# Differential heads weighed in pairs: one run of 24 score matmuls and one pool of six PSUM banks

## Chip, cores and metric

The kernel runs on one core of one Trainium2 chip. The metric is the device time of one execution in microseconds (us). Before the change it is 2826.71 us, the median of 3 runs (2826.54 to 2827.23).

## What is computed

A bidirectional encoder of two layers over 256 tokens of width 2048, batch 1, all in float32. Each layer does this (shortened from the reference):

```
h = rmsnorm(x, g_mix[i]);  z = h @ w_in[i]
dq, dk, dv, cq, ckv, kr, ga, gb = split(z)

# A: differential attention, 8 heads, two maps of width 64 per head
scores  = einsum('bqhcd,bkhcd->bhcqk', dq, dk) * 64 ** -0.5
probs   = softmax(scores)
weights = probs[:, :, 0] - lam * probs[:, :, 1]
od      = rmsnorm(weights @ dv, g_subln[i]) * (1 - lam_init)

# B: latent attention, 8 heads: q from cq, k and v from ckv, a shared rotary key
om = softmax((q_nope k_nope + q_rope k_rope) * 192 ** -0.5) @ v_mla

m = sigmoid(ga) * (od @ w_branch_diff[i]) + sigmoid(gb) * (om @ w_branch_mla[i])
x = x + m @ w_out[i]
x = x + swiglu(rmsnorm(x)) ;  x = x + sigmoid(rmsnorm(x) @ w_ple_gate[i]) * (p[i] @ w_ple_in[i])
```

A last RMSNorm follows the two layers.

## The kernel before

**Products.** Nearly all the time goes into products of a 128-column strip of weights with the 256 tokens. A product (`product`, lines 227 to 236) has 16 chunks where its input is 2048 wide. For each chunk `emit` (216 to 225) issues two TensorE matmuls: line 219 takes the high part of the weights against 512 columns (the high and the low part of the input side by side), line 223 the low part against the 256 columns of the high part. The weights come by DMA in pieces of 128x1024; ScalarE rounds the high part out of a piece (`whi`, line 194) and VectorE subtracts it for the low part (`wlo`, also line 194, shown under line 76, the helper's). Three buffers of each part let the pieces run ahead of TensorE. A product accumulates in one PSUM bank of the pool `ps_mm`; ScalarE copies its second half out (`join`, line 249) and VectorE adds the first half to it (`joined`, 247 to 252). That add frees the bank.

**PSUM.** [...] Before the change `ps_mm` has four for the products, `ps_s` two for the scores, `ps_at` two for everything small (transposes, the products with the values, norms).

**The differential stage**, once per layer. For a head, `queries_keys` (563 to 571) makes a query and a key product, rotates and splits them. `scores` (413 to 422) then multiplies both maps of a head: a map is 64 wide, so its matmuls use 64 of the array's 128 rows, and the loop alternates between the maps, which lie on the two halves of the rows. Two maps, two query blocks and three terms (high and low parts) make 12 matmuls of 64x256 per head, into two banks. `exps` (424 to 432) reads each bank: a VectorE maximum, a small scaling, two ScalarE exponentials with their sums, a VectorE reciprocal. `diff_weights` (674 to 683) joins the two maps into one tile `E` of weights; `E` and `E1` have two buffers each. `diff_out` (685 to 696) transposes the weights on TensorE (`turned`, 434 to 445, line 439), copies them out, and multiplies by the values (line 691).

**Order.** `pipelined` (709 to 718) goes head by head: a step of the filling work, the scores and weights of head h+1, the transposes of head h, another step, the product with the values of head h. The filling work is the generator `beside` (616 to 636): the short products of `keys_up` (two chunks each, in pairs) in turn with `queries_keys` of heads 2 to 7, then `queries_up`, gates, and the norms of the heads (`settle`). The text is a program order only: a planner (the scheduler of the Tile framework) orders each engine's queue by that priority and by when it takes operands and buffers to be ready, and it puts later products on TensorE while earlier work waits. `tc.keep_in_program_order(m)` ties an instruction behind the one that was written before it for its engine. In a queue everything stays in the planned order.

The latent attention (`mla_weights`, 727 to 734) uses `scores` too, with one map of full height. The end of the kernel (926 to 944) transposes the result through banks of `ps_s`, `ps_mm` and `ps_at`.

Of the kernel before, what the change touches and what calls it, by code (L numbers as in the profile page):

```python
# [15 lines left out]
AF = mybir.ActivationFunctionType  # L16
ALU = mybir.AluOpType
AX = mybir.AxisListType

P = 128  # L20
T = 256
# [3 lines left out]
DH = 8  # L25
# [29 lines left out]
def encoder(ctx, tc, x, p, positions, cols, lams, wq, wk, wv, wcq, wckv, wkr, wga, wgb,  # L55
            w_q_up, w_kn, w_v, w_bd, w_bm, w_out, w_gate, w_up, w_down, w_pin, w_pg, rope_c, out):
    nc = tc.nc
    V, A, PE = nc.vector, nc.scalar, nc.tensor
    PSUM = bass.MemoryType.PSUM
    pool = lambda name, bufs=1, **k: ctx.enter_context(tc.tile_pool(name=name, bufs=bufs, **k))  # L60
# [1 line left out]
    wts = pool("wts")  # L62
    tmp = pool("tmp")
    stat = pool("stat")
    ps_mm = pool("ps_mm", 4, space=PSUM)
    ps_s = pool("ps_s", 2, space=PSUM)
    ps_at = pool("ps_at", 2, space=PSUM)

    def scratch(tag, bufs, n=T):
# [2 lines left out]
    def bank(ps=ps_at, tag="at", name="at", shape=(P, 2 * T)):  # L72
        return ps.tile(list(shape), F32, tag=tag, name=name)
# [4 lines left out]
    def stt(o, a, s, b, op0, op1):  # L78
        return V.scalar_tensor_tensor(out=o, in0=a, scalar=s, in1=b, op0=op0, op1=op1)

    def ts(o, a, s1, s2, op0, op1=ALU.bypass):
        return V.tensor_scalar(out=o, in0=a, scalar1=s1, scalar2=s2, op0=op0, op1=op1)  # L82
# [11 lines left out]
    def operand(t):  # L94
        return t.rearrange("p c t -> p (c t)")
# [24 lines left out]
    halves = rc[:, 4 : 4 + P]  # L120
# [28 lines left out]
    neg_lam = const.tile([P, DEPTH], F32, name="neg_lam")  # L149
    gsub = const.tile([P, DEPTH], F32, name="gsub")  # L150
    lam_s = const.tile([P, DEPTH, 2], F32, name="lam_s")
    lam_in = tmp.tile([P, 2, T], F32, tag="E", name="lam_in", bufs=2).rearrange("p l (f d) -> p l f d", f=4)

# [93 lines left out]
    def joined(acc, o=None):  # L247
        t = scratch("join", 3)
        A.activation(t, acc[:, T:], AF.Copy)  # L249
        o = scratch("a", 4) if o is None else o  # L250
        tt(o, acc[:, :T], t, ALU.add)
        return o
# [113 lines left out]
    krs = [const.tile([P, 2 * T], F32R, name=f"kr{j}") for j in range(2)]  # L366
# [26 lines left out]
    def narrow(src, us):  # L393
# [13 lines left out]
                PE.matmul(acc, both[:, j * P : (j + 1) * P], us[a + j], start=a + j == 0, stop=a + j == NC - 1)  # L407
        return acc

    def three(q, k):  # L410
        return [(q[:, :T], k[:, T:]), (q[:, T:], k[:, :T]), (q[:, :T], k[:, :T])]

    def scores(*maps):


        Ss = [bank(ps_s, "S", "S", (P, 2, T)) for _ in maps]
        for b in range(2):
            for j in range(len(maps[0])):
                for S, pairs in reversed(list(zip(Ss, maps))):
                    q, k = pairs[j]  # L420
                    PE.matmul(S[:, b, :], q[:, b * P : (b + 1) * P], k, start=j == 0, stop=j == len(pairs) - 1)  # L421
        return Ss

    def exps(S, E, scale):

        nm, sm, rs = (stat.tile([P, 2], F32, tag=t, name=t, bufs=4) for t in ("nm", "sm", "rsum"))
        V.tensor_reduce(out=nm, in_=S, axis=AX.X, op=ALU.max, negate=True)
        ts(nm, nm, scale, None, ALU.mult)
        for b in range(2):
            last_exp[0] = A.activation(E[:, b, :], S[:, b, :], AF.Exp, bias=nm[:, b : b + 1], scale=scale, accum_out=sm[:, b : b + 1])  # L430
        V.reciprocal(out=rs, in_=sm)
        return rs

    def turned(W, parts=False):

        tp = bank(shape=(P, 2, T))
        for kb in range(2):
            for b in range(2):
                PE.transpose(tp[:, kb, b * P : (b + 1) * P], W[:, b, kb * P : (kb + 1) * P], ident)  # L439
        wt = [tmp.tile([P, 2, T], F32R if parts else F32, tag="wt", name="wt", bufs=4) for _ in range(1 + parts)]  # L440
        A.activation(wt[0], tp, AF.Copy)
        if not parts:
            return wt[0]
        tt(wt[1], tp, wt[0].bitcast(F32), ALU.subtract)
        return wt

    def head(vals, kb, h):
        return vals[:, kb, h // 4, (h % 4) * P : (h % 4 + 1) * P]

    def weights(tag="E", dt=F32):  # L450
        return tmp.tile([P, 2, T], dt, tag=tag, name=tag, bufs=2)
# [65 lines left out]
    for L in range(DEPTH):  # L517
# [43 lines left out]
        qk = [(ub[h], operand(fa(h, F32R))) for h in range(DH)]  # L561
# [13 lines left out]
        qn, kn, qr = [], [], ub[14:]  # L575
# [40 lines left out]
        def beside():  # L616

            for h in range(2, DH):
                if h < 6:
                    keys_up(2 * h - 4)  # L620
                elif h == 7:
                    rotated(joined(narrow(wkr[L], ua)), crm, srm)
                yield
                queries_keys(h)
                yield
            for n in (8, 0, 2, 10):
                if n == 0:
                    settle(0)
                gate(wga, gate_a, next(todo))
                queries_up(n)  # L630
                yield
            settle(4)
            for n in (4, 6):
                gate(wga, gate_a, next(todo))
                queries_up(n)
            gate(wga, gate_a, next(todo))
# [33 lines left out]
        fill = beside()  # L670
        od, ods = [], ub[:8]
        ssd = stat.tile([P, 2 * DH], F32, tag="ssd", name="ssd", bufs=1)

        def diff_weights(h):
            q, k = qk[h]
            E = [weights(), weights("E1")]
            halves = [slice(c * 64, (c + 1) * 64) for c in range(2)]
            r = [exps(S, e, 0.125) for S, e in zip(scores(*(three(q[d], k[d]) for d in halves)), E)]
            ts(r[1], r[1], neg_lam[:, L : L + 1], None, ALU.mult)
            for b in range(2):  # L680
                A.activation(E[0][:, b, :], E[0][:, b, :], AF.Copy, scale=r[0][:, b : b + 1])
                stt(E[0][:, b, :], E[1][:, b, :], r[1][:, b : b + 1], E[0][:, b, :], ALU.mult, ALU.add)
            return E[0]

        def diff_out(h, W):
            wt = turned(W)
            yield
            o = bank()
            for b in range(2):
                for kb in range(2):  # L690
                    PE.matmul(o[:, b * P : (b + 1) * P], wt[:, kb, b * P : (b + 1) * P], head(vd, kb, h), start=kb == 0, stop=kb == 1)  # L691
            f = fa(h)
            od.append(f[:, 0, :])
            A.activation(od[h], o[:, :T], AF.Copy)
            for b in range(2):
                A.activation(f[:, 1, :P], od[h][:, b * P : (b + 1) * P], AF.Square, accum_out=ssd[:, 2 * h + b : 2 * h + b + 1])
# [12 lines left out]
        def pipelined(weigh, put, heads, step):  # L709
            W = weigh(0)  # L710
            for h in range(heads):
                step()
                nxt = weigh(h + 1) if h + 1 < heads else None
                out = put(h, W)
                next(out)
                step()
                next(out, None)
                W = nxt

        pipelined(diff_weights, diff_out, DH, lambda: next(fill, None))  # L720
        for _ in fill:
            pass
        vm, = (v for v in values(w_v[L], ckv) if v is not None)
# [3 lines left out]
        def mla_weights(h):  # L727
            E = weights()
            t = slice(h % 2 * T, (h % 2 + 1) * T)
            S, = scores(three(qn[h], kn[h]) + [(qr[h // 2][:, t], krs[1][:, t]), (qr[h // 2][:, t], krs[0][:, :T])])  # L730
            r = exps(S, E, MLA_SCALE)
            for b in range(2):
                ts(E[:, b, :], E[:, b, :], r[:, b : b + 1], None, ALU.mult)
            return E
# [48 lines left out]
        for part, (f0, f1) in enumerate(FF_PARTS):  # L783
            for f in range(f0, f1):
# [6 lines left out]
                b = pre.pop(0) if pre else joined(product(w_up[L, f], ub))  # L791
# [43 lines left out]
    parts, banks, tiles_ = {}, {}, {}  # L835
# [4 lines left out]
    for n in ends:  # L840
        parts[n] = [piece(w_pg[L, n][:, a * P : (a + PT) * P], PT) for a in (0, PT)]
        m = banks[n, 0] = bank(ps_mm, "mm", "mm")
# [7 lines left out]
    for n in ends:  # L850
        m = banks[n, 1] = bank(ps_mm, "mm", "mm")
# [40 lines left out]
    def transposed(b, q, into, c0=0, c1=4):  # L892
        for c in range(c0, c1):
            tc.keep_in_program_order(PE.transpose(into[:, c * P : (c + 1) * P], xT[:, 4 * q + c, b * P : (b + 1) * P], ident))  # L894
        return into
# [17 lines left out]
            scaled(o[:, k * 2 * T : (k + 1) * 2 * T], src, col, engine)  # L913
        tc.keep_in_program_order(nc.sync.dma_start(out[b, :, q * 2 * T : (q + len(srcs)) * 2 * T], o))

    def S_bank():
        return operand(bank(ps_s, "S", "S", (P, 2, T)))

    def mm_bank():
        return bank(ps_mm, "mm", "mm")  # L920

    def steps(which, n):
        for _ in range(n):
            tc.keep_in_program_order(next(which))
# [6 lines left out]
    column = factors(0)  # L931
    for which, n in ((column, 2), (third, 1), (column, 2), (second, 1), (column, 1), (second, 1), (column, 1), (third, 1), (column, 1), (third, 1), (column, 1)):
        steps(which, n)
    t0 = [transposed(0, q, get()) for q, get in enumerate((S_bank, S_bank, mm_bank, mm_bank))]
    t1 = [transposed(1, q, mm_bank()) for q in range(2)]
    steps(factors(1), 8)
    t1.append(transposed(1, 2, bank()))
    store(0, 0, t0[:1], cols_[0], (A,))
    with tc.issue_after(gains[-1].ins):
        for q, m in ((1, 1), (2, 2)):  # L940
            store(0, q, t0[q : q + m], cols_[0], (A, A))
    t1.append(transposed(1, 3, S_bank()))
    for q in (0, 2):
        store(1, q, t1[q : q + 2], cols_[1], (V, A))

# [87 lines left out]
```

## Time and profile before

| | |
|---|---|
| median of 3 runs | 2826.71 us |
| span of the profiled execution | 2825.0 us |
| TensorE matmul (PE) busy | 2816.4 us, 16691 instructions |
| TensorE weight load (PEld) busy | 2490.9 us |
| VectorE (DVE) busy | 2079.7 us |
| ScalarE (ACT) busy | 1532.1 us |
| score matmuls of the differential heads (line 421, 64 rows) | 192, from 106.3 to 1610.6 us |

The span goes from the first to the last instruction of one profiled execution; 1.7 us of the median lie outside it. In a timeline row stand the start, the length, the engine, the line, the operation, the tiles written and read, the shape, and how many instructions are merged in the row. Matmuls overlap in the array, so a matmul's own length says less than the step from its start to the next one's start. TensorE's granted clock was 0.999 over the span.

### The profile page before, as it was taken

To read this page: it belongs to the slowest core of one execution; us is meant where nothing else is said; L and a number is where in the kernel's file an instruction comes from. 1 tells how busy PE (TensorE), PEld (TensorE's weight loads), DVE (VectorE), ACT (ScalarE), POOL (GpSimd) and SP (SyncE) were. 2 spreads that over 40 slices of the span, in tenths; PEclk is the share of its full clock that TensorE was granted. 3 is DMA by queue.
4 is the path that set the end of the run, shared out by engine and by line. 5 is a ranking of instruction groups with operands and counts; after the bars stand their busy time and mean duration, and the time that the engine had idled before them with its cause. 6 is when DMAs were issued, how large, how long until landed. Compare 5 with 4: busy or idle time off the path is not lost.

```text
span 2825.0 us, 43996 instructions
## 1 busy us (share of the span) xinstructions
PE 2816.4 (100%) x16691; PEld 2490.9 (88%) x16691; DVE 2079.7 (74%) x3574; ACT 1532.1 (54%) x2556; POOL 1.9 (0%) x15
## 2 busy tenths in 40 slices
PE   9999999999999999999999999999999999999998
PEld 8888988888888888888888889888888888888888
DVE  8998668776666666677869976687766666666777
ACT  7676546554444444455646765465544444444556
POOL 0000000000000000000000000000000000000000
PEclk9999999999999999999999999999999999999999
DMA  7545456666666666566565454566666656656664
GB/s 246 176 160 172 157 186 197 193 194 193 187 199 194 189 195 198 193 193 193 194 193 165 157 173 157 193 198 193 194 192 190 197 194 185 202 195 194 193 193 155
DMA packets 158325, 531.37 MB, mean 188 GB/s; under 512 B 17184, under 2 KB 25376, under 8 KB 158112
## 3 DMA queue, kind: packets, MB, share of 16 engines
q1 hardware_dynamic: 157680, 527.96, 59.0%
q8 instruction: 131, 2.15, 0.3%
q14 instruction: 82, 0.67, 0.1%
q10 hardware_dynamic: 432, 0.59, 0.1%
HBM read 526.39 MB, written 2.10 MB: 187 GB/s over the span
## 4 chain that ended last, share of the span: by engine, by line
PE 100%; DMA 0%; DVE 0%; ACT 0%; DVEq 0%; issue 0%
PE mm L219 61%; PE mm L223 31%; PE S L421 1%; PE mmv L493 1%; PE mmv L491 1%; PE mmv L492 1%; PE at L439 1%; PE at L691 1%; PE at L747 0%; PE mm L838 0%; PE mm L407 0%; PE at L706 0%; DMA gcol<-in_cols 0%; PE mmv L462 0%; PE at L332 0%; PE mm L894 0%
## 5 line engine op out<-in xcount | busy, mean ns | idle before, releaser
L194 ACT ACTIVATE whi<-w 128x1024 fp32r<-128x1024 f32 (+2 forms) x1038 | 1064.2, 1026 | 1227.1 <-issue 593.2
L76 DVE TENSOR_TENSOR wlo<-w,whi 128x1024 fp32r<-128x1024 f32 (+2 forms) x1038 | 1225.7, 1181 | 647.4 <-ACT whi L194 638.6
L219 PE MATMUL mm<-ub,whi 128*128 128x512 f32 x3936 | 1340.5, 389 | 0.0
L219 PE MATMUL mm<-ua,whi 128*128 128x512 f32 x3712 | 1274.1, 390 | 0.0
L223 PE MATMUL mm<-ub,wlo 128*128 128x256 f32 x3936 | 1084.6, 276 | 0.0
L223 PE MATMUL mm<-ua,wlo 128*128 128x256 f32 x3712 | 1027.5, 277 | 0.0
L219 PEld LDWEIGHTS mm<-ub,whi 128*128 128x128 f32 x3936 | 737.7, 188 | 151.8
L219 PEld LDWEIGHTS mm<-ua,whi 128*128 128x128 f32 x3712 | 696.3, 188 | 141.1
L223 PEld LDWEIGHTS mm<-ub,wlo 128*128 128x128 f32 x3936 | 738.8, 188 | 1.3
L223 PEld LDWEIGHTS mm<-ua,wlo 128*128 128x128 f32 x3712 | 697.1, 188 | 2.0
L76 DVE TENSOR_TENSOR a<-mm,join 128x256 f32<-128x256 f32 (+1 forms) x423 | 175.0, 417 | 1.7 <-ACT join L867 1.4
L249 ACT ACTIVATE join<-mm 128x256 f32<-128x256 f32 x452 | 165.2, 367 | 6.4 <-PE mm L223 5.8
L76 DVE TENSOR_TENSOR xT<-xT,mm 128x256 f32<-128x256 f32 x256 | 106.9, 420 | 41.6 <-PE mm L223 37.7
L76 DVE TENSOR_TENSOR a<-a,row 128x256 f32<-128x256 f32 (+1 forms) x209 | 87.8, 423 | 5.9
L76 DVE TENSOR_TENSOR a<-a 128x256 f32<-128x256 f32 x120 | 50.9, 425 | 4.0
L76 DVE TENSOR_TENSOR ua<-a,ua 128x256 fp32r<-128x256 f32 x120 | 50.0, 418 | 1.0 <-ACT ua L257 1.0
L257 ACT ACTIVATE ua<-a 128x256 fp32r<-128x256 f32 x120 | 48.1, 403 | 2.6 <-DVE a L76 2.6
L430 ACT ACTIVATE E<-S,nm 128x256 f32<-128x256 f32 x96 | 44.1, 471 | 8.0 <-DVE nm L82 7.9
L491 PE MATMUL mmv<-whi,ua 128*128 128x512 f32 x124 | 47.1, 392 | 0.0
L492 PE MATMUL mmv<-whi,ua 128*128 128x512 f32 x124 | 46.8, 391 | 0.0
L493 PE MATMUL mmv<-wlo,ua 128*128 128x512 f32 x124 | 41.3, 392 | 0.0
L76 DVE TENSOR_TENSOR ssq<-ssq,sq 128x256 f32<-128x256 f32 x96 | 40.3, 420 | 0.3 <-ACT sq L287 0.3
(212 smaller groups left out, 1215.5 us busy)
## 6 DMA issues: line engine op xcount, KB each, us to landing
w<-in_w_gate SPq DMA_DIRECT2D x176, 512.0 KB, 4.6
w<-in_w_up SPq DMA_DIRECT2D x176, 512.0 KB, 4.7
w<-in_w_down SPq DMA_DIRECT2D x128, 512.0 KB, 4.3
w<-in_wga SPq DMA_DIRECT2D x64, 512.0 KB, 3.8
w<-in_wgb SPq DMA_DIRECT2D x64, 512.0 KB, 3.9
w<-in_w_out SPq DMA_DIRECT2D x64, 512.0 KB, 4.6
w<-in_w_pg SPq DMA_DIRECT2D x64, 512.0 KB, 4.8
w<-in_w_down SPq DMA_DIRECT2D x64, 384.0 KB, 3.7
```

The costliest lines, as they stand in the source:

```text
L76: return V.tensor_tensor(out=o, in0=a, in1=b, op=op)
L194: last_split[:] = A.activation(hi[:, s], w[:, s], AF.Copy), tt(lo[:, s], w[:, s], hi[:, s].bitcast(F32), ALU.subtract)
L219: lead = PE.matmul(acc, hi[:, s], u, start=start, stop=False)
L223: rest = PE.matmul(acc[:, T:], lo[:, s], u[:, :T], start=False, stop=stop)
L249: A.activation(t, acc[:, T:], AF.Copy)
L257: return A.activation(hi, src, AF.Copy), tt(lo, src, hi.bitcast(F32), ALU.subtract)
L421: PE.matmul(S[:, b, :], q[:, b * P : (b + 1) * P], k, start=j == 0, stop=j == len(pairs) - 1)
L430: last_exp[0] = A.activation(E[:, b, :], S[:, b, :], AF.Exp, bias=nm[:, b : b + 1], scale=scale, accum_out=sm[:, b : b + 1])
L439: PE.transpose(tp[:, kb, b * P : (b + 1) * P], W[:, b, kb * P : (kb + 1) * P], ident)
L491: PE.matmul(banks[k][b], xh, hi[:, s], start=c == 0, stop=False)
L492: PE.matmul(banks[k][b], xl, hi[:, s], start=False, stop=False)
L493: last_mm[:] = [PE.matmul(banks[k][b], xh, lo[:, s], start=False, stop=c == n - 1)]
```

## The change

Three things change together.

1. `ps_s` is gone and `ps_mm` has six banks. Score banks are taken from it, as are the banks of the last transposes. The number of banks stays eight.
2. `scores` takes a list of heads. For the differential heads it takes two heads, reserves four banks, and issues the 24 matmuls of 64 rows with the higher head first; each is tied behind the matmul written before it. The latent heads come one at a time as before, without the tie.
3. `diff_weights` does two heads at once, and `pipelined` is replaced there by a loop over pairs: two filling steps, the transposes of both heads, a step, the products with the values of both, a step, then the scores and weights of the next pair. The number and order of the filling steps are the same (four for two heads). `pipelined` stays for the latent heads.

```diff
-    ps_mm = pool("ps_mm", 4, space=PSUM)
-    ps_s = pool("ps_s", 2, space=PSUM)
+    ps_mm = pool("ps_mm", 6, space=PSUM)
     ps_at = pool("ps_at", 2, space=PSUM)
...
+    def mm_bank():
+        return bank(ps_mm, "mm", "mm")
+
+    def S_bank():
+        return mm_bank().rearrange("p (b t) -> p b t", b=2)
...
-    def scores(*maps):
-        Ss = [bank(ps_s, "S", "S", (P, 2, T)) for _ in maps]
-        for b in range(2):
-            for j in range(len(maps[0])):
-                for S, pairs in reversed(list(zip(Ss, maps))):
-                    q, k = pairs[j]
-                    PE.matmul(S[:, b, :], q[:, b * P : (b + 1) * P], k, start=j == 0, stop=j == len(pairs) - 1)
+    def scores(*heads):
+        Ss = [[S_bank() for _ in maps] for maps in heads]
+        for banks, maps in zip(Ss, heads):
+            for b in range(2):
+                for j in range(len(maps[0])):
+                    for S, pairs in reversed(list(zip(banks, maps))):
+                        q, k = pairs[j]
+                        m = PE.matmul(S[:, b, :], q[:, b * P : (b + 1) * P], k, start=j == 0, stop=j == len(pairs) - 1)
+                        if len(heads) > 1:
+                            tc.keep_in_program_order(m)
         return Ss
...
-        def diff_weights(h):
-            q, k = qk[h]
-            E = [weights(), weights("E1")]
+        def diff_weights(h0):
             halves = [slice(c * 64, (c + 1) * 64) for c in range(2)]
-            r = [exps(S, e, 0.125) for S, e in zip(scores(*(three(q[d], k[d]) for d in halves)), E)]
...
+            pairs = [[three(qk[h][0][d], qk[h][1][d]) for d in halves] for h in (h0 + 1, h0)]
+            Ws = []
+            for Ss in scores(*pairs):
+                E = [weights(), weights("E1")]
+                r = [exps(S, e, 0.125) for S, e in zip(Ss, E)]
...
+                Ws.append(E[0])
+            return Ws[::-1]
...
-        pipelined(diff_weights, diff_out, DH, lambda: next(fill, None))
+        Ws = diff_weights(0)
+        for h in range(0, DH, 2):
+            for _ in range(2):
+                next(fill, None)
+            outs = [diff_out(h + j, Ws[j]) for j in range(2)]
+            for part in outs:
+                next(part)
+            next(fill, None)
+            for part in outs:
+                next(part, None)
+            next(fill, None)
+            if h + 2 < DH:
+                Ws = diff_weights(h + 2)
...
-    t0 = [transposed(0, q, get()) for q, get in enumerate((S_bank, S_bank, mm_bank, mm_bank))]
+    t0 = [transposed(0, q, mm_bank()) for q in range(4)]
...
-    t1.append(transposed(1, 3, S_bank()))
+    t1.append(transposed(1, 3, mm_bank()))
```

More of the change, by code (lines that the diff above doesn't have):

```diff
@@ L672, in encoder @@
         ssd = stat.tile([P, 2 * DH], F32, tag="ssd", name="ssd", bufs=1)
-        def diff_weights(h):
-            q, k = qk[h]
-            E = [weights(), weights("E1")]
+        def diff_weights(h0):
             halves = [slice(c * 64, (c + 1) * 64) for c in range(2)]
-            r = [exps(S, e, 0.125) for S, e in zip(scores(*(three(q[d], k[d]) for d in halves)), E)]
[L679 to L683, printed above, removed]
+            pairs = [[three(qk[h][0][d], qk[h][1][d]) for d in halves] for h in (h0 + 1, h0)]
[3 more added lines that the diff above has]
+                r = [exps(S, e, 0.125) for S, e in zip(Ss, E)]
+                ts(r[1], r[1], neg_lam[:, L : L + 1], None, ALU.mult)
+                for b in range(2):
+                    A.activation(E[0][:, b, :], E[0][:, b, :], AF.Copy, scale=r[0][:, b : b + 1])
+                    stt(E[0][:, b, :], E[1][:, b, :], r[1][:, b : b + 1], E[0][:, b, :], ALU.mult, ALU.add)
+                Ws.append(E[0])
+            return Ws[::-1]
         def diff_out(h, W):
@@ L729, in mla_weights @@
             t = slice(h % 2 * T, (h % 2 + 1) * T)
-            S, = scores(three(qn[h], kn[h]) + [(qr[h // 2][:, t], krs[1][:, t]), (qr[h // 2][:, t], krs[0][:, :T])])
+            (S,), = scores([three(qn[h], kn[h]) + [(qr[h // 2][:, t], krs[1][:, t]), (qr[h // 2][:, t], krs[0][:, :T])]])
             r = exps(S, E, MLA_SCALE)
@@ L914, in store @@
         tc.keep_in_program_order(nc.sync.dma_start(out[b, :, q * 2 * T : (q + len(srcs)) * 2 * T], o))
[L916 to L920, printed above, removed]
     def steps(which, n):
```

## Prediction

> **What bounds the kernel now.** I read the page's busy times and its chain first, then the waits of TensorE.
>
> ```profile
> span 2825.0 us, 43996 instructions
> PE 2816.4 (100%) x16691; PEld 2490.9 (88%) x16691; DVE 2079.7 (74%) x3574; ACT 1532.1 (54%) x2556; POOL 1.9 (0%) x15
> PE 100%; DMA 0%; DVE 0%; ACT 0%; DVEq 0%; issue 0%
> PE at L507 <- DVE ones L116: 1.0, 1, 1.0
> PE mmv L462 <- ACT whi L194: 0.4, 1, 0.4
> ```
>
> The chain that ended last is TensorE throughout, and TensorE waited for another engine only twice, 1.4 us in all, both at the start. So no wait is there to be removed. A change gains only what it takes out of TensorE's own steps, and loses only by a wait that it creates. The next view is therefore TensorE's timeline around a run of score matmuls, read by starts.
>
> ```profile
> 105.71 0.28 PE L223 MATMUL mm<-ua,wlo 128*128 128x256 f32 x1
> 105.82 0.39 PE L219 MATMUL mm<-ub,whi 128*128 128x512 f32 x1
> 106.05 0.28 PE L223 MATMUL mm<-ub,wlo 128*128 128x256 f32 x1
> 106.25 0.97 PE L421 MATMUL S<-fa,ub 64*128 64x256 f32 x12
> 107.16 0.50 PE L219 MATMUL mm<-ub,whi 128*128 128x512 f32 x1
> 107.49 0.28 PE L223 MATMUL mm<-ub,wlo 128*128 128x256 f32 x1
> ...
> 106.48 0.51 PE L421 MATMUL S<-fa,ub 64*128 64x256 f32 x6
> 106.59 0.63 PE L421 MATMUL S<-fa,ub 64*128 64x256 f32 x8
> 106.83 0.40 PE L421 MATMUL S<-fa,ub 64*128 64x256 f32 x4
> ...
> L421 PE MATMUL S<-fa,ub x192: 273/277/383, 106.3 to 1610.6; 64*128 64x256 f32 x192
> ```
>
> An undisturbed 256-column matmul (L223) is followed after 0.11 us (105.71 to 105.82), a 512-column one (L219) after 0.23 us (105.82 to 106.05). The twelve score matmuls take 0.91 us to the next product (106.25 to 107.16), less than 12 x 0.11 = 1.32: they go through in twos, one on each half of the rows, so six steps of 0.115, or 0.69, would do. The narrower windows of the same run show those steps, 106.48 to 106.59, then 0.24 for two of them to 106.83. What a run costs beyond its steps is then: entry 0.20 for 0.11; first pair to second 0.23 (106.25 to 106.48) for 0.115; last pair to the product about 0.21 for 0.115 (107.16 less 106.83, less one step); and 0.33 for 0.23 at the product after it. In sum, from 106.05 to 107.49 are 1.44 us where 0.11 + 0.69 + 0.23 = 1.03 would do: **0.41 us for a run**. The row of line 421 has 192 matmuls, so there are 16 runs.
>
> **The change part by part.** *Merging the runs.* Sixteen runs become eight. Where transposes follow a run, the price is a little lower:
>
> ```profile
> 123.56 0.39 PE L219 MATMUL mm<-ua,whi 128*128 128x512 f32 x1
> 123.88 0.98 PE L421 MATMUL S<-fa,ub 64*128 64x256 f32 x12
> 124.79 0.65 PE L439 MATMUL at<-ident,E 128*128 128x128 f32 x4
> 125.20 0.36 PE L223 MATMUL mm<-ua,wlo 128*128 128x256 f32 x1
> ...
> 189.07 0.60 PE L439 MATMUL at<-ident,E 128*128 128x128 f32 x4
> 189.43 0.36 PE L223 MATMUL mm<-ua,wlo 128*128 128x256 f32 x1
> ```
>
> Here entry is 0.32 for 0.23 and the run 0.91 for 0.69; the four transposes take 0.41 where a block that no run precedes takes 0.36: 0.09 + 0.22 + 0.05 = 0.36. Between 0.36 and 0.41 I take 0.38. The join of two heads inside a run should cost nothing, since the array stays in its 64-row form and only the bank changes, as it does at every matmul of a run. Eight runs saved are 8 x 0.38 = **3.0 us**.
>
> [...]
>
> *What is given back.* After the run at 106.25 the products go on a little slower for a while:
>
> ```profile
> 105.14 0.39 PE L219 MATMUL mm<-ua,whi 128*128 128x512 f32 x1
> 105.48 0.39 PE L219 MATMUL mm<-ua,whi 128*128 128x512 f32 x1
> 107.61 0.40 PE L219 MATMUL mm<-ub,whi 128*128 128x512 f32 x1
> 107.96 0.40 PE L219 MATMUL mm<-ub,whi 128*128 128x512 f32 x1
> 116.36 0.40 PE L219 MATMUL mm<-ua,whi 128*128 128x512 f32 x1
> 116.71 0.40 PE L219 MATMUL mm<-ua,whi 128*128 128x512 f32 x1
> ```
>
> A chunk takes 0.34 before the run, 0.35 after it, and still 0.35 at 116.36: 9.1 us at 3%, about 0.27 us. After the run at 123.88 this is missing. Why it sets in I can't read from the trace, so each of the new runs may bring 0 to 0.27 more and lose as much; with more runs followed directly by products (the transposes now come two steps after the scores) I give back 0.3 in all, with bounds of -0.5 and +2.2.
>
> *The order of the work.* The transposes, value products, exponentials and VectorE work keep their number and shape, so they cost nothing new if TensorE is never left without products. No DMA is added or moved past another: the filling steps come in the same order, and SP's and POOL's queues keep theirs. What shifts is when the scores come: those of the lower head wait for the query and key of the higher one. The first matmul of a run is tied behind the last product of that key, which it needs anyway, so the tie alone adds no wait; but if a run did wait on chip, for an operand or for the third bank, everything behind it in TensorE's queue would wait too. What covers the chain from key to scores to weights is the next filling, some 12 us per two steps (at 0.34 us a chunk, 32 chunks of query and key and 4 short ones), as it did before. Price with that cover: nothing; without it, the rivals below.
>
> *The banks and the end.* Outside the runs the products have six banks for four: no gain, since TensorE never waited for one. The last transposes take six banks in turn from one pool instead of two; the same number of banks serves them in the same order, and I cost it at nothing, between -0.5 and +0.5.
>
> **Sum.** Against the profiled execution 2825.0 - 3.0 + 0.3 = 2822.3 us of span; with the 1.7 us that the median of the runs has over that span, 2826.7 - 2.7 = **2824.0 us**. Its own bounds: at best 2826.7 - 3.3 (eight runs at 0.41) - 0.5 (slower stretches gone) - 0.5 (the end) = 2822.4; at worst 2826.7 - 2.9 (eight at 0.36) + 2.2 + 0.5 = 2826.5. 0.2% of the time, about what a measurement can tell from no change, is 5.65 us. All sixteen runs together cost 6.1 us and half of them stay, so the forecast can't leave that band by itself.
>
> **Rivals.** *One: the run does not stay whole.* Four banks of six must be free at its start. If the planner finds two, it fills in products between the two heads, and the array changes form as often as before: saving nil, 2826.7 us. For it: products hold one bank under accumulation and one or two on their way out. Against it: the way out is short (below).
>
> *Two, slower: the products run out of banks.* While scores hold four banks, products have two.
>
> ```profile
> 116.37 0.48 ACT L430 ACTIVATE E<-S,nm 128x256 f32<-128x256 f32 x1
> 120.96 0.64 ACT L249 ACTIVATE join<-mm 128x256 f32<-128x256 f32 x2
> 122.48 0.75 DVE L76 TENSOR_TENSOR a<-mm,join 128x256 f32<-128x256 f32 x2
> ```
>
> The last exponential that reads the scores of 106.25 starts at 116.37, so score banks are held for some 10 us. A bank on its way out takes from its copy (120.96) to the end of the first of the two adds (about 122.9), 1.9 us. A long product (16 x 0.34 = 5.4 us) covers that; a short one of two chunks (0.68 us) does not. If in each of the eight holds a short pair leaves TensorE waiting 1.9 - 0.68 = 1.2 us, that is 9.8 us: 2824.0 + 9.8 = 2833.8. It decides from (5.65 + 2.7) / 8 = 1.04 us a pair. Against it: long products stand beside the short ones in the filling, and the planner can take them first. [...]
>
> *Three, slower: VectorE falls behind.* This stage is its fullest.
>
> ```profile
> 106.00:124.00 18.00, 18.00 (x111) 15.41 (x112) 18.00 (x43) 15.43 (x35) 0.00 (x0) 1.00 0.46 149
> 124.00:150.00 26.00, 26.00 (x174) 23.05 (x175) 24.42 (x62) 19.75 (x53) 0.00 (x0) 1.00 0.54 171
> L427 DVE TENSOR_REDUCE nm<-S 128x2 f32<-128x512 f32 x16 | 10.3, 683 | 0.0
> L79 DVE SCALAR_TENSOR_TENSOR E<-E,rsum,E 128x256 f32<-128x256 f32 x16 | 7.1, 479 | 0.1
> L431 DVE RECIPROCAL rsum<-sm 128x2 f32<-128x2 f32 x16 | 2.5, 160 | 0.5 <-ACT E L430 0.2
> L82 DVE TENSOR_SCALAR nm<-nm 128x2 f32<-128x2 f32 x16 | 2.1, 163 | 0.0
> L82 DVE TENSOR_SCALAR rsum<-rsum,neg_lam 128x2 f32<-128x2 f32 x8 | 1.8, 225 | 0.1
> L194 ACT ACTIVATE whi<-w 128x1024 fp32r<-128x1024 f32 (+1 forms) x46 | 47.6, 1034 | 30.5 <-PE mm L219 22.1 <-issue 6.6 <-ACT join L249 1.0
> ```
>
> The windows' columns are length, then PE, PEld, DVE and ACT busy: DVE is busy 18.00 of 18 us, then 24.42 of 26. The groups (of 106 to 250 us, eight heads) sum to 23.8 us, or 2.98 per head. Two heads at once ask for 2.98 us earlier than before, in a stretch with 26.00 - 24.42 = 1.58 us to spare; if the other 1.40 us falls on the pieces of weights that TensorE needs next, eight pairs lose 11.2 us: 2824.0 + 11.2 = 2835.2, again from 1.04 us a pair on. Against it: ScalarE stood 22.1 us before its weight pieces because TensorE had not freed the last ones, so the pieces are mostly ahead; and the first head's weighing leaves the fullest stretch.
>
> **How the numbers follow.** The forecast has 0.67, rival one 0.13, rival two 0.08, rival three 0.09, and 0.03 stays for a gain over 5.65 us that no row shows. Same is 0.67 + 0.13 = 0.80, slower 0.08 + 0.09 = 0.17, faster 0.03. The range goes from 2822.0 to 2834.0: it holds the forecast, rival one and about half of the slower cases, and leaves out some 0.13.
>
> **What would show it.** Right: about eight groups of 24 matmuls of 64 rows, steps of 0.115 us through the middle of each, late steps only at its ends; TensorE's waits still near 1.4 us; VectorE's and ScalarE's counts unchanged. Rival one shows as runs of 12 with products between; two as TensorE waiting for the adds of `joined`; three as its waiting for `wlo`. A change of several us outside the two differential stages would make the working wrong, whatever the total.

## The result, and the profile after

The changed kernel takes **2891.49 us** (median of 4 runs, 2891.18 to 2892.7) against 2826.97 us for the kernel before (4 runs, 2826.54 to 2827.29) on the same chip. The ratio is 1.0229, 95% interval 1.0217 to 1.0241: slower by 64.5 us, and outside the predicted range.

The page of the changed kernel, its span, busy times and chain:

```profile
span 2889.9 us, 43936 instructions
PE 2833.3 (98%) x16691; PEld 2506.8 (87%) x16691; DVE 2089.3 (72%) x3574; ACT 1535.3 (53%) x2556; POOL 1.9 (0%) x15
PE 97%; DVE 2%; ACT 1%; issue 0%; DVEq 0%; ACTq 0%
```

The span has grown by 64.9 us, and the counts of TensorE, VectorE and ScalarE are what they were. But VectorE and ScalarE have entered the chain, which was TensorE alone. So TensorE now waits, and its waits say where:

```profile
PE mm L427 <- DVE fa L75: 42.1, 8, 6.8
PE at L717 <- DVE ub L78: 5.8, 2, 2.9
```

Line 427 is the score matmul, and there are eight waits, one for each pair of heads: 42.1 us for `fa`, the low part of a key. Two more, 5.8 us, stand before the transposes of `settle` (line 717), which come right before the last pair of a layer. Here is the first pair in TensorE's timeline (some steps left out):

```profile
105.89 0.39 PE L218 MATMUL mm<-ua,whi 128*128 128x512 f32 x1
106.11 0.28 PE L222 MATMUL mm<-ua,wlo 128*128 128x256 f32 x1
113.20 2.93 PE L427 MATMUL mm<-fa,ub 64*128 64x256 f32 x24 [6.82 <-DVE fa L75]
116.06 0.79 PE L218 MATMUL mm<-ub,whi 128*128 128x512 f32 x1
...
116.87 0.63 PE L218 MATMUL mm<-ub,whi 128*128 128x512 f32 x1
...
117.51 0.63 PE L218 MATMUL mm<-ub,whi 128*128 128x512 f32 x1
```

At 106.11 the last matmul of the key product is issued; then TensorE does nothing until the scores start at 113.20. Nothing stands between them, and the products of the filling come only behind the run. What TensorE waits for is the whole way from a product to a split key, in ScalarE's and VectorE's timelines:

```profile
107.27 0.36 ACT L248 ACTIVATE join<-mm 128x256 f32<-128x256 f32 x1
...
112.28 0.42 ACT L256 ACTIVATE fa<-a 128x256 fp32r<-128x256 f32 x1 [3.11 <-DVE a L75]
```

```profile
108.54 0.42 DVE L75 TENSOR_TENSOR a<-mm,join 128x256 f32<-128x256 f32 x1
...
112.72 0.42 DVE L75 TENSOR_TENSOR fa<-a,fa 128x256 fp32r<-128x256 f32 x1 [0.48 <-ACT fa L256]
```

The copy at 107.27, the add at 108.54, then the rotation, for which ScalarE waits 3.11 us, and the two parts of the split at 112.28 and 112.72: seven microseconds that products covered before.

There is a second loss. The run's 24 matmuls take 2.93 us, the first chunk behind it takes 0.81 (116.06 to 116.87) and the next 0.64 (to 117.51), where the prediction's rows have 0.34. The windows (length, busy times, then the granted clock) show why:

```profile
106.00:113.20 7.20, 0.39 (x3) 0.08 (x1) 6.60 (x17) 3.27 (x8) 0.00 (x0) 0.72 0.32 109
113.20:116.20 3.00, 3.00 (x25) 2.77 (x25) 1.30 (x3) 0.00 (x0) 0.00 (x0) 0.50 0.00 0
116.20:120.00 3.80, 3.80 (x13) 3.14 (x14) 1.50 (x6) 3.65 (x11) 0.00 (x0) 0.58 0.00 0
```

TensorE's clock has fallen to 0.50 by the time the scores start, and comes back at about 119.4. All eight runs lie in such a stretch: from the first start of a run to its last are 2.51 to 2.52 us, and no matmul of line 427 with 64 rows is shorter than 0.412 us, where the median of the kernel before is 0.277.

Taken by TensorE's starts, the stage of the differential heads has lost 31.9 us in the first layer and 32.7 in the second, and the rest of the kernel 0.3.

### The profile page after: what moved, and what is told of

It is laid out like the page before. It is cut to its first block, busy times and chain, and to the rows that moved or that the text cites. A ratio compares the mean times of both kernels' runs of the same rounds, so it can differ in the third digit from the quotient of the medians.

```text
span 2889.9 us, 43936 instructions
## 1 busy us (share of the span) xinstructions
PE 2833.3 (98%) x16691; PEld 2506.8 (87%) x16691; DVE 2089.3 (72%) x3574; ACT 1535.3 (53%) x2556; POOL 1.9 (0%) x15
## 4 chain that ended last, share of the span: by engine, by line
PE 97%; DVE 2%; ACT 1%; issue 0%; DVEq 0%; ACTq 0%
PE mm L218 60%; PE mm L222 30%; PE mm L427 1%; PE mmv L499 1%; PE mmv L501 1%; PE mmv L500 1%; DVE wlo L75 1%; PE at L702 0%; PE at L447 0%; DVE a L75 0%; PE at L770 0%; PE mm L861 0%; ACT whi L193 0%; PE mm L406 0%; DVE ub L75 0%; DVE sh L575 0%
## 5 line engine op out<-in xcount | busy, mean ns | idle before, releaser
L427 PE MATMUL mm<-fa,ub 64*128 64x256 f32 x192 | 23.4, 426 | 42.1 <-DVE fa L75 42.1
L438 ACT ACTIVATE E<-mm,nm 128x256 f32<-128x256 f32 x96 | 44.2, 474 | 30.6 <-DVE nm L81 30.5
L427 PEld LDWEIGHTS mm<-fa,ub 64*128 64x128 f32 x192 | 21.1, 324 | 44.6 <-DVE fa L75 44.6
```

The lines of the kernel that those rows point to most:

```text
L427: m = PE.matmul(S[:, b, :], q[:, b * P : (b + 1) * P], k, start=j == 0, stop=j == len(pairs) - 1)
```

## The experiments

Three theories were put up. **A, the pool:** one pool hands its banks out in the order in which the program asks, so a product that is written behind the scores can't be placed before the scores have their four banks, and they take them only when their key is there. Before, scores and products asked different pools, and products went ahead of a head's scores. **B, the tie:** `keep_in_program_order` pins the run behind the key, and all else behind the run. **C, shortage:** with four of six banks taken, two are too few for the products.

**The tie taken out** (of the changed kernel).

```diff
-                        if len(heads) > 1:
-                            tc.keep_in_program_order(m)
```

> The changed kernel without the ties between the score matmuls. Theory A (one pool hands out its banks in the order in which the program asks, so that no product written after the scores can start before the scores have their banks; TensorE then waits for the last key): about 2891 us, eight waits of 2.7 to 6.8 us before the runs as in the changed kernel. Theory B (the tie pins the run behind the last key product): 2824 us, no waits. Theory C (four of six banks taken leave the products too few): about 2891.

Measured: 2891.89 us, ratio 1.0229 (1.0214 to 1.0244). Its waits:

```profile
PE mm L427 <- DVE fa L75: 41.9, 8, 6.8
```

The same eight waits and the same time. B falls: the tie costs nothing and holds nothing.

**The pool alone** (in the kernel before: single heads, no tie).

```diff
-    ps_mm = pool("ps_mm", 4, space=PSUM)
-    ps_s = pool("ps_s", 2, space=PSUM)
+    ps_mm = pool("ps_mm", 6, space=PSUM)
...
-        Ss = [bank(ps_s, "S", "S", (P, 2, T)) for _ in maps]
+        Ss = [bank(ps_mm, "mm", "mm").rearrange("p (b t) -> p b t", b=2) for _ in maps]
```

> The kernel before, one head at a time and no ties, with the two score banks taken from one pool of six. Theory A: slower than before; sixteen waits, each shorter than 6.8 us by the filling step that now stands between key and scores (at most 1.4 us of short products), 3 to 5.5 us each, and a slower clock after them: 2880 to 2940. Theory B: no ties, so 2826.7. Theory C: two banks taken of six leave four, as before: 2826.7.

Measured: 2910.9 us, 1.0299 (1.0282 to 1.0316). TensorE's waits:

```profile
PE mm L420 <- DVE fa L75: 21.9, 8, 4.4
PE at L438 <- DVE E L78: 18.1, 2, 9.0
PE at L690 <- ACT wt L440: 12.9, 9, 1.9
```

Sharing the pool is enough by itself, and costs more than the whole change: scores stand ahead of products sixteen times instead of eight. Eight waits are for the key, the rest has moved to the transposes (line 438) and the products with the values (690). A head takes only two of six banks here and leaves the products four, as many as they had, and no product of lines 218 and 222 waits for an add that frees a bank, so C isn't the reason.

**Pairs weighed two steps of the filling later** (the changed kernel; two steps before the first pair, two fewer about the last).

```diff
+        for _ in range(2):
+            next(fill)
         Ws = diff_weights(0)
...
-            next(fill, None)
             if h + 2 < DH:
+                next(fill)
                 Ws = diff_weights(h + 2)
```

> The changed kernel with each pair weighed two filling steps later (the number of steps is the same). Theories A and B: the query and the key are ready when the scores' turn comes, so the waits before the runs go; 2824 us, less what a split last run costs (0.4 us a layer). Theory C: the score banks are held as long as in the changed kernel, so the waits move to the products; 2834 or more.

Measured: 2840.66 us, 1.005 (1.0035 to 1.0065).

```profile
PE mm L218 <- DVE a L75: 9.9, 4, 2.9
PE mm L427 <- DVE fa L75: 1.1, 2, 0.7
```

With two steps of the filling between a key and its scores, the waits for the key are gone, 42.1 to 1.1 us: what was missing was work ahead of the run. In their place stand four waits of products for an add, 9.9 us, which the changed kernel did not have. That is theory C, real, but a different and smaller loss.

**Three steps later** (the same with one more step at the start, and one fewer about the last pair).

```diff
-        for _ in range(2):
+        for _ in range(3):
```

> As the variant weighed two steps later, but three, so that a long product and not a short pair is written right after the scores. If the four waits of up to 2.9 us for an add there were short products that found only two banks, they go, and the run of 24 keeps its gain: 2824 to 2828 us. If they came from the four banks as such, the waits move to the long products: 2835 to 2842.

Measured: 2837.24 us, 1.0036 (1.0023 to 1.0048).

```profile
PE at L372 <- DVE a L75: 2.6, 2, 1.3
PE mm L222 <- DVE wlo L75: 1.6, 3, 0.8
PE mm L427 <- DVE a L75: 1.4, 2, 0.7
```

The short products no longer wait for a bank, but scores do now (line 427 waits for an add that frees one), and beside them the small product that rotates the shared key (line 372, for its operand) and products whose weight pieces come late. Here the shared pool only moves the shortage about.

**The banks claimed early** (the changed kernel; one matmul of a single column into each of the four score banks, from a constant, so that it needs neither query nor key; the scores overwrite it).

```diff
         Ss = [[S_bank() for _ in maps] for maps in heads]
+        if len(heads) > 1:
+            for S in sum(Ss, []):
+                PE.matmul(S[:, 0, :1], ones, ones[:, 0:1], start=True, stop=True)
```

> The changed kernel, ties kept, with one tiny matmul (128x1, overwritten later) into each score bank that needs no query or key, so that the four banks are handed out at once. Theory A (products queue behind the scores for banks in program order): products now pass, the waits for the key go; what stays is the shortage while four banks are held, longer than in the variant two steps later: 2830 to 2850 us. If the waits have to do with the tie or with the pair as such: 2891.

Measured: 2851.4 us, 1.0087 (1.0073 to 1.0101), 1.4 us above the range expected of A. Its timeline at the place at which the changed kernel stood still (the trace shows each of the four claims as two matmuls):

```profile
106.05 0.95 PE L424 MATMUL mm<-ones 128*128 128x1 f32 x8
106.86 0.47 PE L218 MATMUL mm<-ub,whi 128*128 128x512 f32 x1
...
108.84 0.50 PE L218 MATMUL mm<-ub,whi 128*128 128x512 f32 x1 [1.03 <-DVE a L75]
...
117.08 1.69 PE L430 MATMUL mm<-fa,ub 64*128 64x256 f32 x24
```

Pool, pairs, ties and program order are those of the changed kernel; only the moment at which the scores take their banks is earlier. The products go ahead at 106.86, the run of 24 comes at 117.08, whole, with 1.42 us from its first start to its last, and 40.1 us of the 64.5 are back. This shows theory A. The short products now run into C, as at 108.84: a product of two chunks, then a wait for the add that frees a bank. All its waits:

```profile
PE mm L218 <- DVE a L75: 5.5, 8, 1.0
PE mm L222 <- DVE wlo L75: 2.3, 3, 0.8
PE mm L218 <- ACT whi L193: 2.2, 3, 0.7
PE mm L218 <- ACT E L441: 2.0, 2, 1.1
```

The four rows sum to 12.0 us. The claims cost 8 x (106.86 - 106.05) = 6.5, the merged runs give about 2.5 back (below): 16.0 of the 22.6 us by which its span (2847.6) still exceeds that of before. The other 7 us I have not split.

**The same claim with single heads** (two such matmuls ahead of each differential head's scores, and one ahead of each latent head's, in the kernel with the pool alone).

> One head at a time from one pool of six, as in the variant that changes the pool alone, with one tiny matmul into each of the two score banks ahead of the scores, so that the banks are handed out at once. Theory A: the waits of that variant (2911 us) go, four banks stay for products as before: 2827 to 2835. If the loss there came from sharing in another way, it stays near 2911.

Measured: 2846.77 us, 1.0072 (1.0056 to 1.0087).

```profile
PE mm L218 <- DVE a L75: 6.0, 2, 3.0
PE mm L417 <- ACT E L431: 0.9, 2, 0.6
```

64.1 us less than the pool alone, and no wait for a key, so A holds here too; but the expectation was 12 us too low. The claims ask the same pool in the same order, and in the second row two of them (line 417) wait for a bank themselves. How the rest divides stays open.

**TensorE kept busy through the wait** (the changed kernel; 22 unused matmuls of 128x512 tied ahead of each pair's scores).

```diff
+        if len(heads) > 1:
+            busy = bank()
+            for _ in range(22):
+                tc.keep_in_program_order(PE.matmul(busy, ua[0][:, :P], ua[1], start=True, stop=True))
```

> The changed kernel with 22 extra matmuls of 128x512 (5 us, results not used) tied in ahead of each run, so that TensorE is busy while it waits for the key. If some 17 us of the loss are matmuls at half clock after the waits, they go: about 2875 us, granted clock 0.998. If the matmuls were slow for another reason, 2890 or more.

Measured: 2876.84 us, 1.0177 (1.0161 to 1.0193). In its timeline:

```profile
106.01 5.17 PE L424 MATMUL at<-ua,ua 128*128 128x512 f32 x22
113.01 1.70 PE L431 MATMUL mm<-fa,ub 64*128 64x256 f32 x24 [1.82 <-DVE fa L75]
114.64 0.79 PE L218 MATMUL mm<-ub,whi 128*128 128x512 f32 x1
```

The scores start about as late as before (113.01, after 113.20 in the changed kernel): keeping TensorE busy did not bring the key sooner. But the run now takes 1.63 us to the next product instead of 2.86, the mean granted clock is 0.999 where the changed kernel has 0.989, and the time falls by 14.7 us. So about 15 us of the loss are not waiting but the half clock after it. It may be a little more. The last row still steps slowly, 0.80 us to the next chunk and then 0.64 a chunk, the steps that the changed kernel has at 0.50, so here the clock seems to fall just behind the run; and this kernel has 2.4 us of waits ahead of line 218, where the changed kernel has 0.4. By TensorE's starts, the steps at half clock in the changed kernel are about 17 us longer than the same steps elsewhere, an estimate.

**Pools of their own: two banks for products, four for scores** (the changed kernel; the wide products with the values and some banks of the ends move to the scores' pool, so that two are enough to run at all).

```diff
-    ps_mm = pool("ps_mm", 6, space=PSUM)
+    ps_mm = pool("ps_mm", 2, space=PSUM)
+    ps_s = pool("ps_s", 4, space=PSUM)
```

> The changed kernel, pairs and ties as they are, but four banks for scores and two for products, each in a pool of its own (the wide value products and some banks of the end are taken from the four). Theory A: runs of 24 without a wait before them; 2823 to 2826. Theory B: ties are there, so eight waits and 2891. Theory C: two banks are too few for the products: 2834 or more, with TensorE waiting for the adds that free them.

Measured: 2961.73 us, 1.0473 (1.0454 to 1.0493).

```profile
PE mm L219 <- DVE a L76: 51.0, 23, 6.5
PE mm L219 <- DVE xT L76: 14.2, 20, 1.9
```

The expectation failed: no run waits for a key any more, as A has it, but products wait for their adds in every stage, `xT` among them, which belongs to no differential head. So this run mixes two things, and its control was made: **the kernel before with two banks for products and four for scores**, nothing else changed but where those same wide products and ends take their banks.

> The kernel before, one head at a time, no ties, each pool its own, but two banks for products and four for scores (the wide value products and some banks of the end taken from the four). If the loss of the variant with pools of its own came from two product banks being too few in the whole kernel, this is about as slow, 2930 to 2965 us, with TensorE waiting for the adds that free banks in every stage. If it came from pairing with pools of its own, this stays near 2827.

Measured: 2932.09 us (2 runs, 2925.0 and 2939.19), 1.0373 (1.035 to 1.0396).

```profile
PE mm L219 <- DVE a L76: 26.5, 20, 2.6
```

Two product banks cost 105 us without any pairing. That is most of the 135 us of the run before, which says nothing against A.

**Three banks for products, four for scores, one for the rest** (the changed kernel, otherwise as above).

> The changed kernel with pools of its own, three banks for products, four for scores, one small. Theory A: no waits for keys. Two product banks alone cost some 105 us over the whole kernel; if three are enough, this is 2824 plus the waits at the one small bank (up to 1.5 us where two transposes or two value products follow each other, sixteen places): 2824 to 2850.

Measured: 2864.04 us, 1.0134 (1.0112 to 1.0156).

```profile
PE mm L219 <- DVE a L76: 11.5, 7, 3.1
PE at L451 <- ACT wt L453: 3.9, 2, 2.1
```

Missed as well: three product banks still leave waits for adds, and with one bank for the transposes (line 451) they wait for the copy of the transposes before. TensorE's waits in this kernel make about half of the 37 us that it loses; the rest is not split. The pools of every kernel here come to eight banks. Eight don't give the scores four of their own beside four for the products and two for the rest, unless two of them serve twice:

**Four, two, two, and the pair borrows** (the changed kernel with the pools of the kernel before: the first head of a pair borrows the two banks of `ps_at`, the second has the two of `ps_s`).

```diff
+    ps_s = pool("ps_s", 2, space=PSUM)
...
-        Ss = [[S_bank() for _ in maps] for maps in heads]
+        Ss = [[S_bank(k + 1 < len(heads)) for _ in maps] for k, maps in enumerate(heads)]
```

> The changed kernel, pairs and ties as they are, with the pools of the kernel before (four for products, two for scores, two small): the first head of a pair takes the two small banks, the second the two score banks. Theory A: no product asks the pool that the scores wait in, so no waits; the runs of 24 keep their gain of 3.0 us less 0.3: 2824.0 us, runs of 24 with 0.39 us less per pair than two runs of 12. If pairing itself costs (the order of the work, VectorE's load), above 2829.

Measured: 2828.41 us (11 runs), 1.0004 (0.9996 to 1.0013): no difference from the kernel before that the interval shows, though the median lies 1.4 us above the 2826.98 of that kernel, measured beside it. Runs of 24, pairs, ties and program order are those of the change; only the products' pool is not shared with the scores. That takes 63 us of the 64.5 away, and with it A is shown from both ends. A run in its timeline (the first head's twelve, then the second's):

```profile
122.11 0.98 PE L431 MATMUL at<-fa,ub 64*128 64x256 f32 x12
122.93 0.87 PE L431 MATMUL S<-fa,ub 64*128 64x256 f32 x12
123.73 0.39 PE L223 MATMUL mm<-ua,wlo 128*128 128x256 f32 x1
```

By TensorE's starts, a join of two runs that stood between products saves 0.39 us. But ten of the sixteen runs of before had transposes right behind them, where a run costs 0.36 us in place of 0.41 by the prediction's rows, and here products follow every run: all runs and transposes together save about 2.5 us. The forecast for this kernel was 4.4 us too low. 3.0 of them stand in the first pair of each layer:

```profile
127.81 1.28 ACT L442 ACT_TABLE_LOAD   x1
129.10 0.47 ACT L442 ACTIVATE E<-at,nm 128x256 f32<-128x256 f32 x1
...
133.02 1.09 ACT L194 ACTIVATE whi<-w 128x1024 fp32r<-128x1024 f32 x1
```

ScalarE loads the table of the exponential, 1.28 us, then has eight exponentials in a row for two heads where it had four for one, and the next piece of weights is rounded only at 133.02. TensorE has used up its pieces and loses 0.48 and 1.03 us at two steps, in each layer. Another 0.9 us lie in other steps that are each a little longer.

**The table loaded early** (the last kernel, with one exponential of two columns tied in some 25 us ahead).

```diff
+        soon = stat.tile([P, 2], F32, tag="soon", name="soon", bufs=1)
+        tc.keep_in_program_order(A.activation(soon, ones[:, 0:2], AF.Exp))
```

> The variant with the small banks, and one tiny exponential (two elements, not used) tied behind ScalarE's work for the first key, so that the table of the exponential is loaded some 20 us before the first pair needs it. In the variant with the small banks TensorE lost 3.0 us, all in the first pair of each layer, on pieces of weights that ScalarE rounds after the load (1.28 us) and eight exponentials. If the load is what makes them late, most of that goes and the time is 2825.5 to 2827.0 us; if eight exponentials in a row are enough, it stays at 2828.4.

Measured: 2827.7 us (11 runs), 1.0003 (0.9994 to 1.0012). ScalarE's timeline at the same place:

```profile
102.31 1.28 ACT L627 ACT_TABLE_LOAD   x1
...
129.24 0.47 ACT L442 ACTIVATE E<-at,nm 128x256 f32<-128x256 f32 x1 [0.92 <-DVE nm L82]
...
133.16 1.09 ACT L194 ACTIVATE whi<-w 128x1024 fp32r<-128x1024 f32 x1
```

The load now stands at 102.31, yet the exponentials start no earlier (129.24): ScalarE waits 0.92 us for VectorE's maximum, which the load had hidden, and the weight piece comes at 133.16. So the load did not make that piece late. What is left is the maximum and the eight exponentials in a row, which no run took apart. Of the two waits of TensorE one has gone; the time is 1.0 us above that of the kernel before where it was 1.4, a difference within what two such sets of runs differ. No kernel of the study beats the one before.

## Why the prediction was wrong

**The step that failed** is the one on the order of the work: "What covers the chain from key to scores to weights is the next filling, some 12 us per two steps ... as it did before. Price with that cover: nothing". The filling was there, but it could not be placed ahead of the scores any more: its products ask the same pool, behind them. The changed kernel with early claims (products pass, 40 us come back), the one whose pair borrows (63 us) and the kernel before with the pool alone (84 us lost) show it from three sides. The order moved as well: in the text of the kernel before, a step of the filling (mostly a short one) stood between a head's key and its scores, and now none does. Two steps put there bring 50.8 us back even with one pool, and pools apart bring 63 back even with none. So the loss comes of both together, a shared pool and scores written close behind their key. The text put the price of a shared pool into the number of banks ("six banks for four: no gain") and not into the order in which they are handed out. It also said what would follow "if a run did wait on chip": everything behind it waits too. That is what happened, eight times, and without the tie just the same.

**The price of the lost cover.** 42.1 us before the scores, 5.8 before the transposes of `settle`, and about 15 (by the run that kept TensorE busy) to 17 (by the starts) at half clock: 62.9 to 64.9. Less the 2.5 of the merged runs, as measured where the pair borrows, that is 60.4 to 62.4, of 64.5 measured; what is left, 2 to 4 us, I have not split. The half clock is a term that the prediction didn't have: it had read a granted clock of 1.00 in both windows of before, and asked of no wait what the clock would do after it.

**What bounds the kernel:** right. It gains only by TensorE's own steps and loses by waits that are made; outside the two stages only 0.3 us moved.

**Merging the runs:** right in its mechanism. 3.0 us were worked out, eight joins at 0.38; where the pair borrows, a join between products gave 0.39, but all runs and transposes together about 2.5, since runs that had ended at transposes now end at products.

**Given back:** 0.3 was taken with bounds to 2.2; the other steps that got slightly longer came to 0.9 where the pair borrows. That is within the bounds; with the first pairs' 3.0 it uses up the gain.

**Rival one,** the run torn apart: it did not happen; all eight runs have 24 matmuls without a product between.

**Rival two,** too few banks: not the cause of this loss, but real. Its mechanism appears when the runs come later: four waits, 9.9 us, where 9.8 were worked out, though from eight of 1.2 us. In the changed kernel the same wait came back eight times through PSUM, 42.1 us in all, but by the order in which banks were handed out. Two banks fewer under scores (the pool alone) did not cure it, and an early claim in the same six banks did.

**Rival three,** weight pieces late: not in the changed kernel, where no product waits for `wlo`. Where the pair borrows it is real in the first pair of each layer alone, 3.0 us in place of 11.2, and there VectorE's piece is late because ScalarE's comes behind the exponentials.

## What to carry to other kernels

When two users are put into one pool, ask not only how many banks each needs, but in which order they will ask, and what the first asker waits for: whoever asks behind it waits as well, even with banks free. Count the work that stands between a producer and its consumer after such a change as if nothing could pass. And price a wait on the engine that bounds the kernel at more than its length: here the half clock behind 47.9 us of waits cost another 15 or more.

## What the runs showed of the hardware

**The clock can fall after a short wait, and after its end.** Where the pairs come two steps later, TensorE's windows are these, about three waits of 2.91, 2.17 and 2.16 us that end at 125.37, 158.86 and 1569.14:

```profile
122.00:126.00 4.00, 1.09 (x7) 0.73 (x6) 4.00 (x14) 3.97 (x10) 0.00 (x0) 1.00 0.41 135
126.00:130.00 4.00, 4.00 (x15) 3.43 (x15) 3.58 (x13) 4.00 (x17) 0.00 (x0) 0.57 0.37 123
...
159.00:163.00 4.00, 4.00 (x24) 3.51 (x25) 3.71 (x13) 4.00 (x17) 0.00 (x0) 1.00 0.28 85
...
1570.00:1574.00 4.00, 4.00 (x16) 3.44 (x16) 3.72 (x13) 4.00 (x17) 0.00 (x0) 0.57 0.35 119
```

During the first wait the clock is 1.00, and it falls to 0.50 only at about 126.5, when TensorE has been working again for 1.1 us. After the second it doesn't fall; after the third, which is no longer, it does. Where single heads claim their banks, it stays at 1.00 even behind a wait of 2.98 us that ends at 112.26:

```profile
112.20:117.00 4.80, 4.74 (x27) 4.17 (x28) 4.16 (x14) 4.73 (x14) 0.00 (x0) 1.00 0.34 111
```

So the length of a wait alone doesn't decide. Away from the end of the kernel, a stretch at 0.50 in the changed kernel lasts 3.41 us once, twice that (6.83) five times and three times that (10.24) twice. In the clock records of that kernel the four stretches of the first layer begin at 109.15, 150.11, 184.25 and 225.21: 40.96, 75.09 and 116.05 us after the first, or 12, 22 and 34 times 3.41. What sets these lengths and beginnings, no run here shows. The waits of 2.91 and 2.16 us that a fall followed are shorter than the shortest of these stretches.
